# The output projection of a hybrid decoder layer as seven half products, with factors made in the merge

## The chip, the cores and the metric

The kernel runs on one core of a Trainium2 chip. Its work is done by TensorE (PE in the profile; PEld is its weight load), VectorE (DVE), ScalarE (ACT) and GpSimd (POOL); SyncE (SP) issues most DMAs. The metric is the time of one execution on the device in microseconds (us).

## The reference

One decoder layer over 512 tokens of width 1024: an mLSTM branch and a sliding-window attention branch read the same normalised input; their outputs are merged under gates, projected, and added to x. Then come an MLP and a gated embedding.

```
y_a = sigmoid(o_ml) * h_ml                     # mLSTM branch
y_b = swa_with_sinks(...)                      # attention branch
merged = sigmoid(g_a) * (y_a @ w_branch_a) + sigmoid(g_b) * (y_b @ w_branch_b)
x = x + merged @ w_out                         # the output projection
u = rmsnorm(x, norm_mlp_g) @ w_up
x = x + square(relu(u)) @ w_down
gate = sigmoid(rmsnorm(x, norm_ple_g) @ w_ple_gate)
x = x + gate * (p @ w_ple_proj)
return rmsnorm(x, final_norm_g)
```

All of it is in float32. The change concerns the line with w_out, the merge ahead of it, and the transposes of x behind it.

## The kernel before

A product of float32 matrices is made of three matmuls: each operand is split into a high part in a rounded format (fp32r) and the remainder, and high times high, high times low and low times high are summed in PSUM. `split` (L134 and L135) does it: ScalarE casts the high part, VectorE subtracts it from the operand to get the remainder. `load_w` loads 128x1024 of weights through SP (L143) and splits them into `wh` and `wl`. A matmul has 128 rows and columns of weights and 512 columns of moving data.

**The mLSTM branch ends** with four heads' value products (L784), which read the value tiles `vm`. `ya_of` multiplies a head's transposed outputs by the output gates, which `gate_of` loads from HBM by SP (`gl` from `god`, L619), and splits them into `ya`. The products of w_b with the attention branch run between; their results lie in `t2` (`gb` in the profile).

**The merge** has eight products of w_a with `ya`, one for each 128 channels and all 512 tokens, of 24 matmuls each. The results go to two PSUM tiles in turn (`psg`). VectorE multiplies each by its gate (L850, into `sga`), POOL adds the attention part (L851), and the sum is split into `mg`, high and low (L134, L135).

**The output projection** comes after the PSUM pools of the branches are closed and new ones opened. SP loads x there, four tiles of 128 tokens (`xk`, L864). For each half of the 1024 output columns, four chunks of w_out come in, and each is multiplied for four token tiles by six matmuls: 2 x 4 x 4 x 6 = 192, into `psp` and `psg`. After each half, VectorE adds the results to `xk` (L895), and `columns_of` transposes four columns of 128 of it (four 128x128 transposes on PE for each, L877) and splits them with the norm's gain (ScalarE L137, VectorE L138) into `x1`. Each column has a PSUM tile of two banks (`pair`) to itself, of which it uses one.

**Then** `up` multiplies w_up with `x1`, after ScalarE has begun to square `xk` for the norm (`junk`, L916). The down projection behind it already works by quarters: seven products in place of eight block products, from four quarters of the weights and of the activations and from sums of them.

The order of the work isn't the order of the program text: a scheduler places each instruction on its engine's queue ahead of time, and an engine runs its queue strictly in that order. A tile with several buffers hands out a slot again when its last user is done, and the next user waits for that.

## Time and profile before

| | us |
| --- | --- |
| three runs | 904.98, 906.15, 906.18 |
| median | 906.15 |
| the profiled execution | 905.84 |
| its span | 904.1 |
| PE busy | 890.4 |
| DVE busy | 627.0 |
| ACT busy | 466.9 |
| POOL busy | 28.1 |

Times in rows of the timeline count from the start of the span. A row gives start, length, engine, line, operation, the tile written and those read, the shape, and in brackets the engine's idle time ahead of it with what ended it. Where PE works without a gap, its row of two or more matmuls is as long as its modelled pipeline; the spacing of starts is what one costs. Against the span of 904.1, the whole execution has 1.74 us around it. The merge with w_a lies from 413 to 460, the output projection from 460 to 507 and `up` and `down` behind it.

### The profile page before, as it was taken

The page shows a single profiled execution, that of the slowest core. Times are in us where ns is not written, and L with a number is a line of the kernel's source. Part 1 is how long each engine was busy: PE and PEld are TensorE (multiplying, and loading weights), DVE is VectorE, ACT ScalarE, POOL GpSimd, SP SyncE. Part 2 cuts the span into 40 slices and gives each one's busy share as a digit, 9 for nine tenths or more (in the row PEclk, how much of TensorE's full clock was granted, in tenths as well). Part 3 has the DMA queues.
Part 4 walks back from the last instruction along what each step waited for, and adds up shares of the span by engine and source line. Part 5 has one row for each costly group of instructions (what it writes and reads, how often), then busy time and mean ns, then how long its engine had stood idle before and what let it go on. Part 6 is the DMA issues. An engine that isn't in the chain of part 4 may idle for free.

```text
span 904.1 us, 11781 instructions
## 1 busy us (share of the span) xinstructions
PE 890.4 (98%) x4500; PEld 741.6 (82%) x4500; DVE 627.0 (69%) x1016; ACT 466.9 (52%) x778; POOL 28.1 (3%) x47
## 2 busy tenths in 40 slices
PE   8999999999999999999999999999999999999996
PEld 7888899998877677777878888888888888888786
DVE  6884687874787977557644568856965795689556
ACT  6473444443676667664322555345535543554753
POOL 2021000000000000001210000000000000000000
PEclk9999999999999999999999999999999999999999
DMA  7753134435121132234452620631262044101402
GB/s 259 252 159 125 47 116 157 149 122 168 61 70 52 43 117 71 94 103 150 144 187 94 228 74 2 209 119 45 68 212 94 1 162 161 49 24 50 160 1 94
DMA packets 30347, 101.52 MB, mean 112 GB/s; under 512 B 4301, under 2 KB 4813, under 8 KB 30290
## 3 DMA queue, kind: packets, MB, share of 16 engines
q1 hardware_dynamic: 28002, 93.15, 31.0%
q0 software_dynamic: 2144, 7.35, 2.3%
q8 instruction: 35, 0.57, 0.3%
q10 hardware_dynamic: 144, 0.26, 0.1%
q14 instruction: 22, 0.18, 0.1%
HBM read 91.30 MB, written 8.40 MB: 110 GB/s over the span
## 4 chain that ended last, share of the span: by engine, by line
PE 73%; ACT 2%; DVE 2%; DMA 1%; issue 0%; SPq 0%; ACTq 0%
PE psg L162 42%; PE psp L162 22%; PE pst L784 2%; PE pst L713 1%; PE psa L705 1%; PE pst L774 1%; PE psa L162 1%; PE psa L668 1%; PE psa L669 1%; DMA gfin<-in_g_fin 1%; PE psp L877 1%; ACT jk L796 1%; ACT wh L134 1%; ACT pT L707 0%; DMA ptok<-in_p 0%
## 5 line engine op out<-in xcount | busy, mean ns | idle before, releaser
L135 DVE TENSOR_TENSOR wl<-wr,wh 128x1024 fp32r<-128x1024 f32 x134 | 170.7, 1279 | 131.0 <-ACT wh L134 124.4
L134 ACT CAST wh<-wr 128x1024 fp32r<-128x1024 f32 x134 | 140.9, 1053 | 208.5 <-PE psg L162 85.6
L162 PE MATMUL psg<-x,wh 128*128 128x512 f32 x512 | 157.9, 389 | 0.0
L162 PE MATMUL psp<-wh,uf 128*128 128x512 f32 x448 | 139.2, 390 | 0.0
L162 PEld LDWEIGHTS psg<-x,wh 128*128 128x128 f32 x512 | 96.0, 188 | 19.8
L162 PE MATMUL psg<-h,wh 128*128 128x512 f32 x320 | 101.3, 395 | 0.0
L162 PE MATMUL psg<-x,wl 128*128 128x512 f32 x256 | 99.6, 389 | 0.0
L162 PEld LDWEIGHTS psp<-wh,uf 128*128 128x128 f32 x448 | 84.1, 188 | 17.4
L162 PE MATMUL psp<-wl,uf 128*128 128x512 f32 x224 | 87.2, 390 | 0.0
L134 ACT CAST wh<-wd 128x1024 fp32r<-128x1024 f32 x44 | 46.3, 1055 | 60.4 <-PE psp L162 23.2
L162 PEld LDWEIGHTS psg<-h,wh 128*128 128x128 f32 x320 | 58.7, 188 | 15.9 <-issue 4.9
L135 DVE TENSOR_TENSOR wl<-wd,wh 128x1024 fp32r<-128x1024 f32 x44 | 53.3, 1220 | 17.6 <-ACT wh L134 17.4
L162 PE MATMUL psg<-h,wl 128*128 128x512 f32 x160 | 62.8, 393 | 0.0
L162 PEld LDWEIGHTS psg<-x,wl 128*128 128x128 f32 x256 | 48.1, 188 | 10.0
L162 PE MATMUL psa<-h,wh 128*128 128x256 f32 (+1 forms) x256 | 55.1, 311 | 0.2 <-ACT p L593 0.2
L162 PEld LDWEIGHTS psp<-wl,uf 128*128 128x128 f32 x224 | 42.0, 188 | 8.7
L135 DVE TENSOR_TENSOR uf<-F,uf 128x1792 fp32r<-128x1792 f32 (+2 forms) x20 | 33.0, 1652 | 21.8 <-ACT uf L134 21.8
L162 PEld LDWEIGHTS psa<-h,wh 128*128 128x128 f32 x256 | 41.8, 190 | 3.7 <-ACT p L593 0.9
L162 PE MATMUL psg<-yb,wh 128*128 128x512 f32 x128 | 42.7, 408 | 0.0
L162 PE MATMUL psg<-ya,wh 128*128 128x512 f32 x128 | 40.7, 394 | 0.0
L162 PE MATMUL psa<-h,wl 128*128 128x256 f32 (+1 forms) x128 | 39.6, 309 | 0.0
L134 ACT CAST uf<-F 128x1792 fp32r<-128x1792 f32 (+2 forms) x20 | 28.0, 1399 | 19.3 <-DVE F L951 19.2
(284 smaller groups left out, 1667.7 us busy)
## 6 DMA issues: line engine op xcount, KB each, us to landing
wr<-in_w_up SPq DMA_DIRECT2D x32, 512.0 KB, 3.2
wd<-in_w_down SPq DMA_DIRECT2D x24, 512.0 KB, 3.3
wr<-in_w_o SPq DMA_DIRECT2D x8, 512.0 KB, 4.8
gd<-gr POOLq DMA_DIRECT2D x8, 512.0 KB, 3.2
wr<-in_w_qsw SPq DMA_DIRECT2D x8, 512.0 KB, 4.0
wr<-in_w_qkml SPq DMA_DIRECT2D x8, 512.0 KB, 3.3
wr<-in_w_b SPq DMA_DIRECT2D x8, 512.0 KB, 3.2
gl<-gd SPq DMA_DIRECT2D x8, 512.0 KB, 3.4
```

The source lines that it names most:

```text
L134: A.copy(dst[0], src)
L135: V.tensor_sub(dst[1], src, r32(dst[0]))
L162: last_mm[0] = T.matmul(ps, l, r, start=first and i == 0, stop=last and i == len(ops) - 1, skip_group_check=parts)
L668: T.matmul(o, q[:, n * P : (n + 1) * P], kk[kp][ab][:, k0 : k0 + 256], start=True, stop=False)
L669: T.matmul(o, q[:, n * P : (n + 1) * P], kl[kp][ab][:, k0 : k0 + 256], start=False, stop=True)
L705: T.transpose(pt[:, c : c + P], lm3[ab][:, g, j * P : (j + 1) * P], ident)
L713: T.matmul(o[HALF[ab], :], vs[n + 1 - nk + j][:, c : c + 64], pTs[j][:, ab * 512 : (ab + 1) * 512], start=j == 0, stop=j == nk - 1,)
L774: T.matmul(psc[:, n0:], qk[4 + h][:, n0 : n0 + P], qk[h][:, n0:], start=True, stop=True)
L784: T.matmul(pn[:, : DV + 1], wT[s][:, t * P : (t + 1) * P], vm[s][:, h, :], start=s == 0, stop=s == t)
L796: A.activation(jk[:, :DV], h_of(h, t), AF.Square, scale=rd[:, t : t + 1], accum_out=hss[:, h, t : t + 1])
L877: T.transpose(ps[:, m * P : (m + 1) * P], xk[m][:, k * P : (k + 1) * P], ident)
```

## The change

The output projection is written as seven products of halves, as in the down projection. `merged` is seen as four blocks, two halves of the tokens by two halves of the channels of each pair; w_out as four quarters b11, b12, b21, b22. For each pair of merged results (the even one holds A21 and A11 as its two token halves, the odd one A22 and A12), the merge now makes the sums S1 = A21 + A22, S2 = S1 − A11, S3 = A11 − A21 and S4 = A12 − S2, and splits A11, A22 with A12, S1 with S2 and S3 with S4. Four sums of quarters are made in place (b12 from b22 and b12, and so on), each for both halves kh of the channels. Each product then has 24 matmuls: two token tiles, four pairs of channels in two halves, three matmuls each with 512 columns. X, Y and Z are PSUM tiles that take A11 and A12; S2, S3 and A22; S1 and S4. ScalarE copies X after A11 (`p1`). VectorE adds X, Y, Z and `p1` to `xk` as they are done, eighteen additions of 128x512 in place of eight.

The x tiles (`xk`) now take over the slots of the value tiles (tag `tk`, moved to a pool that lives on), and their loads are issued ahead of the merge. b11 and b12 lie in `lm`, b21 in `pT`, b22 in `wr`. The PSUM pools are closed only after the projection. `columns_of` takes its PSUM from the caller: `two_columns` puts two columns into one tile of two banks. The calls for columns 0 to 3 stand inside the last product (S4 with b22), those for 4 to 7 behind it. The host lays w_out out by quarters. The remaining code is the same; line numbers are higher by one before the change, and by 92 behind it.

On SP, where the last output gates are loaded (`gl`) ahead of the merge, before:

```order
L143 DMA wr_4301<-in_w_a 128x1024
L619 DMA gl_4032<-god_466 128x1024
L619 DMA gl_4052<-god_467 128x1024
L143 DMA wr_4341<-in_w_a 128x1024
L619 DMA gl_4098<-gd_1834 128x1024
```

and after:

```order
L144 DMA wr_4304<-in_w_a 128x1024
L144 DMA wr_4360<-in_w_a 128x1024
L859 DMA xk_4077<-in_x 128x1024
L859 DMA xk_4078<-in_x 128x1024
L859 DMA xk_4079<-in_x 128x1024
L859 DMA xk_4080<-in_x 128x1024
L620 DMA gl_4035<-god_469 128x1024
L620 DMA gl_4055<-god_470 128x1024
L144 DMA wr_4396<-in_w_a 128x1024
```

The four x loads and one load of w_a have moved ahead of the two gate loads.

On DVE, in the middle of the merge, two products' steps before (`sga` is a merged result, `gl` its gate, `wl` and `mg` are remainders):

```order
L850 TENSOR_TENSOR sga_4175<-psg_4144,gl_4176 128x512
L135 TENSOR_TENSOR wl_4304<-wr_4301,wh_4303 128x1024
L135 TENSOR_TENSOR mg_4181<-sga_4175,mg_4180 128x512
L850 TENSOR_TENSOR sga_4215<-psg_4184,gl_4176 128x512
L135 TENSOR_TENSOR wl_4344<-wr_4341,wh_4343 128x1024
L135 TENSOR_TENSOR mg_4219<-sga_4215,mg_4218 128x512
```

and after, behind the third product's multiplication (L865, sga_4208) and a sum of quarters (L932), up to the fifth's multiplication (`ms` are the sums S1 to S4, `wl_4466` the remainder of a quarter of w_out):

```order
L136 TENSOR_TENSOR mg_4156<-sga_4208,mg_4155 128x256
L865 TENSOR_TENSOR sga_4244<-psg_4213,gl_4209 128x512
L136 TENSOR_TENSOR wl_4399<-wr_4396,wh_4398 128x1024
L136 TENSOR_TENSOR mg_4250<-sga_4244,mg_4249 128x512
L887 TENSOR_TENSOR ms_4253<-sga_4208,sga_4244 128x256
L888 TENSOR_TENSOR ms_4253<-ms_4253,sga_4208 128x256
L136 TENSOR_TENSOR mg_4258<-ms_4253,mg_4257 128x512
L892 TENSOR_TENSOR ms_4254<-sga_4208 128x256
L893 TENSOR_TENSOR ms_4254<-sga_4244,ms_4253 128x256
L136 TENSOR_TENSOR wl_4466<-wq_4069,wh_4465 128x1024
L136 TENSOR_TENSOR mg_4264<-ms_4254,mg_4263 128x512
L865 TENSOR_TENSOR sga_4298<-psg_4267,gl_4299 128x512
```

From one pair's first multiplication to the next pair's there are thirteen steps in place of six.

On ACT, at the projection's end, before, with the last four columns of `x1` (`x_799` is its high part):

```order
L916 ACTIVATE junk_4712,ss_4713<-xk 128x1024
L916 ACTIVATE junk_4717,ss_4718<-xk 128x1024
L137 ACTIVATE x_799_4392<-psp_4675,gmlp 128x512
L137 ACTIVATE x_799_4392<-psp_4682,gmlp 128x512
L137 ACTIVATE x_799_4392<-psp_4689,gmlp 128x512
L916 ACTIVATE junk_4722,ss_4723<-xk 128x1024
L137 ACTIVATE x_799_4392<-psp_4696,gmlp 128x512
```

and after, with all eight (`x_831` is the high part, and of the tiles 4703 holds columns 0 and 1, 4723 columns 2 and 3, 4743 columns 4 and 5, 4756 columns 6 and 7):

```order
L138 ACTIVATE x_831_4457<-psa_4703,gmlp 128x512
L138 ACTIVATE x_831_4457<-psa_4723,gmlp 128x512
L138 ACTIVATE x_831_4457<-psa_4703,gmlp 128x512
L1008 ACTIVATE junk_4784,ss_4785<-xk_4077 128x1024
L138 ACTIVATE x_831_4457<-psa_4723,gmlp 128x512
L1008 ACTIVATE junk_4789,ss_4790<-xk_4078 128x1024
L138 ACTIVATE x_831_4457<-psa_4743,gmlp 128x512
L138 ACTIVATE x_831_4457<-psa_4756,gmlp 128x512
L1008 ACTIVATE junk_4794,ss_4795<-xk_4079 128x1024
```

The squares for the norm stand between the copies of the columns, and two columns of a tile are copied one after the other, with others between. On PE all 32 transposes now stand ahead of the first `up` matmul; before, the last four of them stood ten matmuls behind it.

The diff:

```diff
--- before.py
+++ after.py
@@ -77,6 +77,7 @@
     wp = pool(ctx, "wp")
     bp = pool(ctx, "bp")
     ap = pool(st_a, "ap")
+    xp = pool(ctx, "xp", side="right")
     c1 = pool(st_s, "c1", side="right")
     sp = pool(st_s, "sp", side="right")
     pp = pool(st_p, "pp", space=PSUM)
@@ -117,7 +118,7 @@
         return hl, [[t[:, k, :] for t in hl] for k in range(KT)]
 
     def tk(n):
-        return sp.tile([P, NH * (DV + 1)], F32, tag="tk", bufs=4, name=nm(n))
+        return xp.tile([P, NH * (DV + 1)], F32, tag="tk", bufs=4, name=nm(n))
 
     def tok_scratch(n="lm"):
         return sp.tile([P, D], F32, tag="lm", bufs=LMB, name=nm(n))
@@ -842,59 +843,150 @@
     ya_of(3)
 
 
-    mg = []
-    for i in range(8):
+
+
+    def load_quarter(c, pool_, tag, bufs):
+        t = pool_.tile([P, 1024], F32, tag=tag, bufs=bufs, name=nm("wq"))
+        nc.sync.dma_start(out=t, in_=w_out[c])
+        return t
+
+    b11 = [load_quarter(4 * kh, sp, "lm", LMB) for kh in range(2)]
+    b12 = [load_quarter(4 * kh + 1, sp, "lm", LMB) for kh in range(2)]
+
+
+    xk = [tk("xk")[:, :D] for _ in range(NT)]
+    for m in range(NT):
+        nc.sync.dma_start(out=xk[m], in_=x[m * P : (m + 1) * P, :])
+
+    def merged(i):
         ps = ps_g()
         mm_T(ps, load_w(w_a[i], KT * P, KT), ya)
         sg = act_f("sga")
         V.tensor_mul(sg, ps, gate_of(gad, i))
         G.tensor_tensor(sg, sg, t2[i], ALU.add)
-        m_ = act_hl("mg")
-        split(m_, sg)
-        mg.append(m_)
-
-
-    st_s.close()
-    st_p.close()
-    xp = pool(ctx, "xp", side="right")
-    pp = pool(ctx, "pq", space=PSUM)
-    XK = xp.tile([P, NT, D], F32, name="xk")
-    xk = [XK[:, m, :] for m in range(NT)]
-    for m in range(NT):
-        nc.sync.dma_start(out=xk[m], in_=x[m * P : (m + 1) * P, :])
-
-    def pair():
-
-        return pp.tile([P, 2, 512], F32, tag="pair", bufs=3, name=nm("psp"))
-
-    def ps_g():
-        return pp.tile([P, 512], F32, tag="g", bufs=2, name=nm("psg"))
-
-    def columns_of(dst, k, g):
-
-        ps = pair()[:, 0, :]
+        return sg
+
+    halves_of = lambda t: [t[:, :256], t[:, 256:]]
+
+    mf = []
+    for i in range(4):
+        even, odd = merged(2 * i), merged(2 * i + 1)
+        a21, a11 = halves_of(even)
+        a22, a12 = halves_of(odd)
+        if i % 2 == 0:
+            own = act_hl("mg")
+        part = [halves_of(t)[i % 2] for t in own]
+        split(part, a11)
+        f = {"A11": part}
+        hl = act_hl("mg")
+        split(hl, odd)
+        f["A22"], f["A12"] = zip(*[halves_of(t) for t in hl])
+        t12, t34 = act_f("ms"), act_f("ms")
+        s1, s2 = halves_of(t12)
+        s3, s4 = halves_of(t34)
+        V.tensor_add(s1, a21, a22)
+        V.tensor_sub(s2, s1, a11)
+        hl = act_hl("mg")
+        split(hl, t12)
+        f["S1"], f["S2"] = zip(*[halves_of(t) for t in hl])
+        V.tensor_sub(s3, a11, a21)
+        V.tensor_sub(s4, a12, s2)
+        hl = act_hl("mg")
+        split(hl, t34)
+        f["S3"], f["S4"] = zip(*[halves_of(t) for t in hl])
+        mf.append(f)
+
+    b22 = [load_quarter(4 * kh + 3, wp, "wr", WRB) for kh in range(2)]
+    b21 = [load_quarter(4 * kh + 2, sp, "pT", 2) for kh in range(2)]
+
+    def halves_a():
+        t = ps_a()
+        return [t[:, :512], t[:, 512:]]
+
+    def columns_of(dst, k, g, ps):
+
         for m in range(NT):
             T.transpose(ps[:, m * P : (m + 1) * P], xk[m][:, k * P : (k + 1) * P], ident)
         split(dst[k], ps, g[:, k : k + 1])
 
 
+    def out_proj():
+        X, Y, Z = halves_a(), halves_a(), [ps_t(), ps_t()]
+
+        def form(raw):
+            return load_w(None, 1024, 2, raw)
+
+        def prod(ps, a, w, kh, first, last, toks=range(2)):
+            for t in toks:
+                ops = []
+                for k in range(2):
+                    ops += pairs([h[:, t * P : (t + 1) * P] for h in mf[2 * kh + k][a]], [h[:, k, :] for h in w])
+                chain(ps[t], ops, first and kh == 0, last and kh == 1, True)
+
+        def acc(ps, toks, n, part=range(2)):
+            for t in part:
+                o = xk[2 * toks + t][:, n * 512 : (n + 1) * 512]
+                V.tensor_add(o, ps[t], o)
+
+        for kh in range(2):
+            V.tensor_sub(b12[kh], b22[kh], b12[kh])
+        for kh in range(2):
+            prod(X, "A11", form(b11[kh]), kh, True, False)
+            V.tensor_add(b11[kh], b12[kh], b11[kh])
+        own = [act_f("p1") for _ in range(2)]
+        for t in range(2):
+            A.copy(own[t], X[t])
+        for kh in range(2):
+            prod(Y, "S2", form(b11[kh]), kh, True, False)
+        acc(Y, 1, 1)
+        for kh in range(2):
+            prod(X, "A12", form(b21[kh]), kh, False, True)
+            V.tensor_sub(b21[kh], b21[kh], b11[kh])
+        acc(X, 1, 0)
+        for kh in range(2):
+            prod(Y, "S3", form(b12[kh]), kh, False, False)
+        acc(Y, 0, 1)
+        acc(own, 0, 1)
+        for kh in range(2):
+            V.tensor_sub(b11[kh], b22[kh], b11[kh])
+            prod(Z, "S1", form(b11[kh]), kh, True, False)
+        acc(Z, 0, 1)
+        acc(own, 1, 1)
+        acc(own, 0, 0)
+        for kh in range(2):
+            prod(Y, "A22", form(b21[kh]), kh, False, True)
+        acc(Y, 0, 0)
+
+        w = [form(b22[kh]) for kh in range(2)]
+        prod(Z, "S4", w[0], 0, False, True)
+        two_columns(0)
+        prod(Z, "S4", w[1], 1, False, True, [0])
+        acc(Z, 1, 1, [0])
+        two_columns(2)
+        prod(Z, "S4", w[1], 1, False, True, [1])
+        acc(Z, 1, 1, [1])
+        two_columns(4)
+        two_columns(6)
+
     x1b, x1 = big_hl("x1")
-    for nh in range(2):
-        if nh == 0:
-            a, b = pair(), pair()
-            pv = [a[:, 0, :], a[:, 1, :], b[:, 0, :], b[:, 1, :]]
-        else:
-            a = pair()
-            pv = [a[:, 0, :], a[:, 1, :], ps_g(), ps_g()]
-        for c in range(4):
-            w = load_w(w_out[nh * 4 + c], 2 * 512, 2)
-            for m in range(NT):
-                mm_tok(pv[m], w, mg[2 * c : 2 * c + 2], m, first=c == 0, last=c == 3)
-        for m in range(NT):
-            o = xk[m][:, nh * 512 : (nh + 1) * 512]
-            V.tensor_add(o, pv[m], o)
-        for k in range(4):
-            columns_of(x1, 4 * nh + k, gmlp)
+
+    def two_columns(k):
+        two = halves_a()
+        for i in range(2):
+            columns_of(x1, k + i, gmlp, two[i])
+
+    out_proj()
+
+    st_s.close()
+    st_p.close()
+    pp = pool(ctx, "pq", space=PSUM)
+
+    def pair():
+
+        return pp.tile([P, 2, 512], F32, tag="pair", bufs=3, name=nm("psp"))
+
+    def ps_g():
+        return pp.tile([P, 512], F32, tag="g", bufs=2, name=nm("psg"))
 
 
 
@@ -1056,10 +1148,10 @@
 
     x2b, x2 = big_hl("x2")
     for k in range(4):
-        columns_of(x2, k, gple)
+        columns_of(x2, k, gple, pair()[:, 0, :])
     ple(0, wp0)
     for k in range(4, 8):
-        columns_of(x2, k, gple)
+        columns_of(x2, k, gple, pair()[:, 0, :])
     evicted = ple(1, load_w(w_pp[1], 2 * 512, 2))
     rk = []
     fs = cp.tile([P, NT, 4], F32, name="fs")
@@ -1208,7 +1300,7 @@
         "w_gb": _halves(w[:, 5640:6664]),
         "w_a": _t_form(i["w_branch_a"][0]),
         "w_b": _t_form(_heads(i["w_branch_b"][0].T).T),
-        "w_out": _tok_form(i["w_out"][0], 2, 512),
+        "w_out": _quarters(i["w_out"][0]),
         "w_up": _t_form(i["w_up"][0]),
         "w_down": np.concatenate([_quarters(down[q * 1024 : (q + 1) * 1024]) for q in range(4)], axis=0),
         "w_pg": _tok_form(i["w_ple_gate"][0], 2, 512),
```

More of the change, by code (lines that the diff above doesn't have):

```diff
@@ new lines, in block_kernel @@
+    b22 = [load_quarter(4 * kh + 3, wp, "wr", WRB) for kh in range(2)]
[4 more added lines that the diff above has]
+    def columns_of(dst, k, g, ps):
+        for m in range(NT):
+            T.transpose(ps[:, m * P : (m + 1) * P], xk[m][:, k * P : (k + 1) * P], ident)
+        split(dst[k], ps, g[:, k : k + 1])
+    def out_proj():
[50 more added lines that the diff above has]
+        two_columns(6)
```

5 lines of the change are left out of this document (1 added, 4 removed).

## The prediction

> **What bounds the kernel now.** I read the engines and the chain of waits on the profile's page first, then busy time by stage, then PE's timeline where the stages meet. The page:
>
> ```profile
> span 904.1 us, 11781 instructions
> PE 890.4 (98%) x4500; PEld 741.6 (82%) x4500; DVE 627.0 (69%) x1016; ACT 466.9 (52%) x778; POOL 28.1 (3%) x47
> PE 73%; ACT 2%; DVE 2%; DMA 1%; issue 0%; SPq 0%; ACTq 0%
> ```
>
> PE is busy 98% of the span and holds most of the chain. The three stages below are the merge, the output projection and a stretch of the down projection, which already has seven products (columns: stretch, its length, then busy time of PE, PEld, DVE, ACT, POOL, granted clock, DMA share, GB/s).
>
> ```profile
> 413.00:460.30 47.30, 46.26 (x211) 37.38 (x208) 34.17 (x36) 16.70 (x22) 9.93 (x7) 1.00 0.48 156
> 460.30:507.00 46.70, 46.63 (x216) 38.31 (x216) 19.54 (x22) 11.99 (x16) 1.29 (x1) 1.00 0.41 145
> 551.00:590.00 39.00, 39.00 (x174) 32.30 (x173) 32.28 (x35) 18.76 (x20) 0.00 (x0) 1.00 0.40 135
> ```
>
> All three are PE's. In the projection VectorE (DVE) has more than half its time free; in the merge it is taken for 34 of 47 us. The clock is 1.00 throughout. PE around the projection:
>
> ```profile
> 460.37 0.47 PE L162 MATMUL psp<-wh,mg 128*128 128x512 f32 x1 [0.88 <-ACT wh L134]
> ...
> 461.60 0.62 PE L162 MATMUL psp<-wh,mg 128*128 128x512 f32 x2
> 462.28 0.62 PE L162 MATMUL psp<-wh,mg 128*128 128x512 f32 x2
> ...
> 506.08 1.60 PE L877 MATMUL psp<-ident,xk 128*128 128x128 f32 x12
> 507.44 0.71 PE L162 MATMUL psg<-x,wh 128*128 128x512 f32 x2
> ```
>
> Three matmuls take 462.28 − 461.60 = 0.68 us, so one 0.2267. PE waits 0.88 us once, at the stage's start, and nowhere at its end: twelve transposes from 506.08 to 507.44 (0.113 each) and the first up product follows.
>
> **The change, part by part.**
>
> *Fewer products.* 192 matmuls become 7 × 24 = 168 of the same shape: −24 × 0.2267 = −5.44 us. All of it is on PE, which is the path.
>
> *PSUM not reopened.* The 0.88 us wait is put down to the weight cast, but the first projection matmul writes PSUM tiles that only exist once the old pools are closed, and the last reader of those is the multiplication at 459.53 (below), which ends at 460.22. Now the pools stay open until the projection is over and the first product needs only early factors: −0.88.
>
> *The merge has more VectorE work.* Its steps now, by DVE and POOL:
>
> ```profile
> 423.69 0.69 DVE L850 TENSOR_TENSOR sga<-psg,gl 128x512 f32<-128x512 f32 x1 [0.86 <-PE psg L162]
> 424.55 2.36 DVE L135 TENSOR_TENSOR wl<-wr,wh 128x1024 fp32r<-128x1024 f32 x1 [0.16 <-ACT wh L134]
> 426.83 0.68 DVE L135 TENSOR_TENSOR mg<-sga,mg 128x512 fp32r<-128x512 f32 x1
> 427.43 0.68 DVE L850 TENSOR_TENSOR sga<-psg,gl 128x512 f32<-128x512 f32 x1
> 428.03 1.21 DVE L135 TENSOR_TENSOR wl<-wr,wh 128x1024 fp32r<-128x1024 f32 x1
> ...
> 459.53 0.69 DVE L850 TENSOR_TENSOR sga<-psg,gl 128x512 f32<-128x512 f32 x1 [1.65 <-PE psg L162]
> ```
> ```profile
> 424.54 1.29 POOL L851 TENSOR_TENSOR sga<-sga,gb 128x512 f32<-128x512 f32 x1 [216.55 <-ACT wh L134]
> 428.19 2.20 POOL L851 TENSOR_TENSOR sga<-sga,gb 128x512 f32<-128x512 f32 x1 [2.37 <-DVE sga L850]
> ```
> ```profile
> 553.80 0.42 DVE L948 TENSOR_TENSOR F<-F 128x256 f32<-128x256 f32 x1
> 554.26 0.42 DVE L950 TENSOR_TENSOR F<-F 128x256 f32<-128x256 f32 x1
> 558.23 1.22 DVE L997 TENSOR_TENSOR wd<-wd,wd 128x1024 f32<-128x1024 f32 x1
> 559.36 1.22 DVE L135 TENSOR_TENSOR wl<-wr,wh 128x1024 fp32r<-128x1024 f32 x1
> ```
>
> Two things are read here. Steps in a row cost about 0.09 less than they last: 0.60 for 128x512 (427.43 to 428.03), 1.13 for 128x1024 (558.23 to 559.36); so 0.34 for 128x256, and 0.46 where one uses the other's result. And the POOL addition and a VectorE step on two SBUF inputs don't run together: the later one is held for all of the other (2.36 instead of 1.22 at 424.55, 2.20 instead of 1.29 at 428.19). The Trainium skill, page "SBUF — State Buffer", section "SBUF: two separate sides", says the same more strictly: the port pair that VectorE and GpSimd share is an exclusive lock, held for the whole instruction by whichever came first. These rows agree with it; by that rule the sum is the one below, and without it some 3.8 us less.
>
> A product of 24 matmuls takes PE 5.44 us, a pair 10.88. Of a pair VectorE has before two multiplications, two weight remainders and two merge remainders: 2 × (0.60 + 1.13 + 0.60) = 4.7. Now it has two multiplications 1.20, three remainders of factors on 512 columns 1.80 and one on 256 0.34, four sums 1.60, two weight remainders 2.26 and a sum of quarters 1.13: 8.3. Three holes lie between them, since the steps stand in one fixed order: after each multiplication the remainder needs the POOL addition (which is held behind a 1024-wide step) and then ScalarE's cast, about 1.6 and 2.0 us after what VectorE has to do meanwhile, and S1/S2 need a cast, 0.8. That makes 12.8 a pair against PE's 10.88. The first pair, with both weight remainders held by POOL as at 424.55, brings the third multiplication to about 436.7 instead of 432.3 (459.53 − 5 × 5.44) and the fifth, 12.8 later, to 449.3. Product six (counted from zero) writes the PSUM tile that the fifth multiplication reads, of two; its turn on PE comes two products ahead of the last multiplication, at 459.53 − 2 × 5.44 = 448.65 less the 0.2 from its last matmul, and it gets the tile at 449.9 to 450.1: +1.5. Bounds: 0 if the holes fill, 3.9 if the second pair loses 4.3 like the first and not 1.9.
>
> *Waits inside the projection.* VectorE's work there is fourteen remainders of weights (three of them up's) and four sums of quarters, 18 × 1.13 = 20.3, sixteen accumulations into x, 9.6, the last pair's steps, 4.9, and a first column, 0.7: 35.5 of about 41 us, against 19.54 of 46.7 in the row above. Queue order then decides. (a) S2's second half needs the last pair's S2 remainder, which stands behind one more weight remainder. PE gets there at 450.0 + 10.88 + 5.44 (A11) + 2.72 (S2's first half) + 1.13 (five matmuls) = 470.2; VectorE multiplies for the last pair at about 461.2, and from there to the end of that remainder its steps and holes are 9.6: 470.8, +0.6. (b) A12 writes the tile that ScalarE copies first; both copies stand behind a weight cast and a factor's cast: +0.7. (c) S3's first weight remainder: +0.15. (d) A22's weight remainder stands behind eight accumulations, 8 × 0.60 = 4.8 us, of the 5.44 that the product ahead of it lasts: +0.8. Together +2.3. The down stage with its 32.28 of 39.00 has no PE wait, so the lower bound is 0; the upper one is 5, where the 35.5 us get the holes of a merge pair, 4.4, twice and not once.
>
> *The left columns.* x1's 32 transposes now write two columns into one two-bank tile, and all of them stand ahead of up; four columns are done inside the last product.
>
> ```profile
> 487.18 0.75 DVE L138 SCALAR_TENSOR_TENSOR x<-psp,gmlp,x 128x512 fp32r<-128x512 f32 x1 [0.15 <-ACT x L137]
> ...
> 505.60 1.06 ACT L916 ACTIVATE junk<-xk 128x1024 f32<-128x1024 f32 x1 [3.70 <-PE psg L162]
> 506.66 1.04 ACT L916 ACTIVATE junk<-xk 128x1024 f32<-128x1024 f32 x1
> 507.70 1.82 ACT L137 ACTIVATE x<-psp,gmlp 128x512 fp32r<-128x512 f32 x3
> 510.47 0.69 ACT L137 ACTIVATE x<-psp,gmlp 128x512 fp32r<-128x512 f32 x1
> ```
>
> The second column's transposes wait for the split of the first in the same tile; columns 4 and 6 wait for those of 1 and 3. ScalarE's order at the end is copies of 0, 2, 1, square, 3, square, 4, 6, square, 5, square, 7. The last transposes (column 7) need column 6 split. From the start of copy 1: copies 0.57 × 3 = 1.71 ((1.82 − 0.69)/2 each), two squares 2.12, the last copy 0.69, a handover 0.15, VectorE's 0.75, a handover 0.1: 5.5 us. PE has in that time two matmuls and 16 transposes, 0.45 + 1.8 = 2.25. So it waits 3.3 in all, in pieces of about one us; +3.4 with the other handovers. Bounds: 1.1 without the squares between, 4.4 if the third square comes ahead as well. What the up products are late by is not caught up later, since nothing behind them waits on anything but PE.
>
> *x earlier.* The four x loads move ahead of two gate loads in SP's queue, and can start only when the value tiles were last read:
>
> ```profile
> 403.82 3.30 PE L784 MATMUL pst<-vm,dm 128*128 128x257 f32 x14 [0.17 <-DVE hd L788]
> ```
> ```profile
> 413.48 1.64 SPq L619 DMA_DIRECT2D gl<-god  x2
> ...
> 460.25 1.75 SPq L864 DMA_DIRECT2D xk<-in_x  x4
> ```
> ```profile
> 411.00:414.00 3.00, 2.94 (x17) 2.17 (x16) 2.64 (x8) 1.31 (x2) 0.00 (x0) 1.00 0.00 0
> 414.00:417.00 3.00, 2.84 (x17) 2.44 (x18) 3.00 (x5) 1.24 (x2) 0.00 (x0) 1.00 0.73 213
> 462.00:464.00 2.00, 2.00 (x10) 1.65 (x10) 1.34 (x2) 0.31 (x1) 0.00 (x0) 1.00 1.00 383
> ```
>
> The values are free at 407.1. 2.1 MB at the 383 GB/s of the last row take 5.5 us, and first bytes come about 1.5 us after the issue (460.25 against 462): done at 414.2. The gate loads are issued at 413.48 in both kernels, their bytes due at 415.0: 0, covered by DMA engines that are idle (share 0.00) up to there. The spare is 0.8 us. The quarters' early loads lie in tiles that are free by then and likewise cost nothing; if they were late, the first sum of quarters would be, on VectorE.
>
> **Sum.** −5.44 − 0.88 + 1.5 + 2.3 + 3.4 = +0.9 on the profiled run's 905.84 (span 904.1), so 906.7. That run is 0.3 below the median of the three, 906.15.
>
> **Rivals.** Less than 0.2% (1.8 us) can't be told from no change here, so up to 904.3 counts as faster and from 908.0 as slower.
>
> *VectorE keeps up* (ends faster). POOL's additions fall between VectorE's two-input steps instead of on them, the fifth multiplication is done by 448.5 and the waits a to d go with it; only the end stays: 905.84 − 5.44 − 0.88 + 3.4 = 902.9. For it: the down stage carries 32 of 39 without a wait. Against: the rows at 424.55 and 428.19; and a product now leaves VectorE 5.44 − 0.69 − 2.36 − 0.68 = 1.7, which the new work, (8.3 − 4.7)/2 = 1.8, fills without the holes.
>
> *x delays the gates* (ends slower). If the four loads run at the 213 GB/s of 414 to 417 instead of 383, they take 9.8 us, end at 418.5, and the output gates for the last heads, ya and the merge come 3.5 later: 910.2. It decides once the loads end after 415.0. Against: 213 has 1 to 1.5 us of start-up in it.
>
> *No overlap of VectorE's steps* (ends slower). If a step costs its whole duration whenever it waits for the one before, two pairs of 13 steps lose 26 × 0.09 = 2.3 more by product six, and 0.8 more by A22: 909.8. For it: the factor sums use each other, 0.46 instead of 0.34. Against: 0.60 and 1.13 in the rows, between different tiles.
>
> **How the numbers follow.** My sum has chance 0.50, with a range of its own of 903.7 to 909.7: the bounds of the three plus terms together give 900.6 (0 + 0 + 1.1) and 912.8 (3.9 + 5 + 4.4), and I go halfway. 0.05 of it is faster, 0.36 within, 0.09 slower. VectorE keeps up: 0.22, faster. x delays the gates: 0.10, slower. No overlap: 0.15, of which 0.02 within. The 0.03 left are slower (several waits at once). So faster 0.27, same 0.38, slower 0.35. The range 902.3 to 910.0 leaves out about a third of the first rival (below), two thirds of the second and a quarter of the third: 0.07 + 0.07 + 0.04.
>
> **What would show it.** The number of projection matmuls falls by 24 and no wait of 0.88 is left at the first; a wait of PE on the multiplication (L865) at about 448.5, of 1.5 us; POOL additions of 2.2 to 2.3; waits of 0.6 to 0.8 at 470, 473 and 490; some 3 us of waits in the transposes (L909) ahead of up; gate loads at 413.5 as before; and up to down as long as now. I am wrong if PE doesn't wait on L865 in the merge, if the waits in the transposes add up to under 1.5 or over 4.5, or if the first sy multiplication moves.

## The result

| | us |
| --- | --- |
| the kernel before, 22 runs beside the changed one | 905.67 (904.38 to 906.69) |
| the changed kernel, 22 runs | 907.45 (904.75 to 909.06) |
| ratio | 1.0018, 95% interval 1.0011 to 1.0025 |
| the changed kernel's profiled execution | 907.43, span 905.7 |

The change makes the kernel slower by 0.18%, some 1.8 us, just inside what the prediction called no change, and 0.75 us above its 906.7. An eighth of the projection's matmuls, 24 of 192 or 5.4 us of PE time, is gone, and all of it and a little more is given back.

The page of the changed kernel says where: PE has 4.4 us less to do, VectorE 26.6 us more, and PE's share of the chain of waits falls from 73% to 66% while VectorE's rises from 2% to 6%.

```profile
span 905.7 us, 11804 instructions
PE 886.0 (98%) x4476; PEld 736.1 (81%) x4476; DVE 653.6 (72%) x1064; ACT 476.5 (53%) x794; POOL 31.4 (3%) x47
PE 66%; DVE 6%; ACT 3%; DMA 1%; issue 1%; POOL 1%; POOLq 0%; ACTq 0%; SPq 0%; DVEq 0%
```

The chain of waits of the stretch from 407 to 515 us, by line, of the kernel before and then of the changed one:

```profile
by line: PE psg L162 56.5%; PE psp L162 30.6%; PE psp L877 3.5%; ACT jk L796 2.3%; PE pst L824 1.8%; DVE hs L805 1.0%; ACT wh L134 1.0%; DVE sy L825 0.7%; issue 0.5%; DVE gb L814 0.4%; ACT hs L787 0.4%; ACT sd L274 0.3%; PE pst L784 0.2%; D
```
```profile
by line: DVE wl L136 14.4%; PE psg L163 11.7%; DVE mg L136 7.4%; DVE xk L929 6.2%; POOL sga L866 5.2%; PE psa L163 5.1%; PE pst L163 4.7%; issue 4.3%; DMA gl<-god 4.0%; ACT mg L135 3.7%; DVE sga L865 3.5%; PE psa L909 2.5%; ACT jk L797 2.3%
```

Before, the path runs almost wholly through PE. After, it leaves PE in the merge and runs through weight remainders (`wl`), merge remainders (`mg`), accumulations into x (`xk`) and POOL's additions, up to the product A22.

PE's timeline of the changed kernel shows every place at which it waits for them, and the start of `up`:

```profile
450.99 0.70 PE L163 MATMUL psg<-ya,wh 128*128 128x512 f32 x2 [1.44 <-DVE sga L865]
...
471.81 0.74 PE L163 MATMUL psa<-wh,mg 128*128 128x512 f32 x2 [0.35 <-DVE mg L136]
...
474.16 0.50 PE L163 MATMUL psa<-wh,mg 128*128 128x512 f32 x1 [0.44 <-ACT p L938]
...
491.73 0.50 PE L163 MATMUL psa<-wl,mg 128*128 128x512 f32 x1 [0.60 <-DVE wl L136]
...
503.76 0.40 PE L163 MATMUL pst<-wh,mg 128*128 128x512 f32 x1
...
505.69 0.63 PE L909 MATMUL psa<-ident,xk 128*128 128x128 f32 x4 [0.74 <-DVE ss L1009]
506.87 0.66 PE L909 MATMUL psa<-ident,xk 128*128 128x128 f32 x4 [0.55 <-DVE x L139]
508.49 1.32 PE L909 MATMUL psa<-ident,xk 128*128 128x128 f32 x8 [0.96 <-DVE x L139]
509.56 0.71 PE L163 MATMUL psg<-x,wh 128*128 128x512 f32 x2
```

The idle times in brackets count from the end of the modelled pipeline; by starts each wait is some 0.16 us longer (the first one is 450.99 − 449.16 − 0.23 = 1.60, where 449.16 is the matmul ahead). From the last projection matmul at 503.76 to `up` at 509.56 there are 5.8 us, of which twenty transposes and the last matmul account for 20 x 0.113 + 0.23 = 2.5: 3.3 us of waits.

VectorE's timeline of the merge has the three holes, and POOL's the additions that are held:

```profile
437.52 0.68 DVE L865 TENSOR_TENSOR sga<-psg,gl 128x512 f32<-128x512 f32 x1
...
440.96 0.42 DVE L136 TENSOR_TENSOR mg<-sga,mg 128x256 fp32r<-128x256 f32 x1 [1.62 <-ACT mg L135]
...
444.97 0.69 DVE L136 TENSOR_TENSOR mg<-sga,mg 128x512 fp32r<-128x512 f32 x1 [1.84 <-ACT mg L135]
...
447.15 0.69 DVE L136 TENSOR_TENSOR mg<-ms,mg 128x512 fp32r<-128x512 f32 x1 [0.69 <-ACT mg L135]
...
450.16 0.68 DVE L865 TENSOR_TENSOR sga<-psg,gl 128x512 f32<-128x512 f32 x1
```
```profile
438.35 2.13 POOL L866 TENSOR_TENSOR sga<-sga,gb 128x512 f32<-128x512 f32 x1 [8.48 <-DVE sga L865]
442.12 2.16 POOL L866 TENSOR_TENSOR sga<-sga,gb 128x512 f32<-128x512 f32 x1 [1.64 <-DVE sga L865]
```

A pair takes VectorE 450.16 − 437.52 = 12.64 us. And one wait that the sum had put at nothing, in SP's and VectorE's rows:

```profile
406.24 1.75 SPq L859 DMA_DIRECT2D xk<-in_x  x4
413.81 0.33 SPq L620 DMA_DIRECT2D gl<-god  x1
```
```profile
418.24 1.41 DVE L826 SCALAR_TENSOR_TENSOR sy<-pst,gml,gl 128x512 f32<-128x512 f32 x2 [0.81 <-DMA gl<-god]
```

The same multiplication began at 417.01 in the kernel before, without a wait.

Between marks that both traces have, the account is this (marks: the first product with `ya`, the merge's first multiplication, the first projection matmul, the first `up` product, the first `down` product):

| stretch | before | after | difference |
| --- | --- | --- | --- |
| first `ya` product to first multiplication | 10.70 | 11.27 | +0.57 |
| to the first projection matmul | 36.68 | 37.35 | +0.67 |
| to `up` | 47.07 | 47.58 | +0.51 |
| to `down` | 44.14 | 43.62 | −0.52 |
| together | 138.59 | 139.82 | +1.23 |

The spans differ by 1.6 us; 0.37 of it lies ahead of the first mark. Most of the −0.52 in the last row is no gain: in the kernel before four of the 32 transposes stand inside `up`, after the change all stand ahead of it, 4 x 0.113 = 0.45.

### The profile page after: what moved, and what is told of

Its sections match the earlier page's. It is cut to its first block, busy times and chain, and to the rows that moved or that the text cites. A ratio compares the mean times of both kernels' runs of the same rounds, so it can differ in the third digit from the quotient of the medians.

```text
span 905.7 us, 11804 instructions
## 1 busy us (share of the span) xinstructions
PE 886.0 (98%) x4476; PEld 736.1 (81%) x4476; DVE 653.6 (72%) x1064; ACT 476.5 (53%) x794; POOL 31.4 (3%) x47
## 4 chain that ended last, share of the span: by engine, by line
PE 66%; DVE 6%; ACT 3%; DMA 1%; issue 1%; POOL 1%; POOLq 0%; ACTq 0%; SPq 0%; DVEq 0%
PE psg L163 37%; PE psp L163 19%; PE pst L785 2%; DVE wl L136 2%; PE psa L163 2%; PE pst L714 1%; PE psa L706 1%; PE pst L775 1%; PE psa L669 1%; DVE mg L136 1%; PE psa L670 1%; DMA gfin<-in_g_fin 1%; DVE xk L929 1%; POOL sga L866 1%; PE pst L163 1%
## 5 line engine op out<-in xcount | busy, mean ns | idle before, releaser
L136 DVE TENSOR_TENSOR wl<-wr,wh 128x1024 fp32r<-128x1024 f32 x126 | 155.4, 1238 | 109.0 <-ACT wh L135 99.0
L135 ACT CAST wh<-wr 128x1024 fp32r<-128x1024 f32 x126 | 132.2, 1051 | 177.2 <-PE psg L163 65.4
L135 ACT CAST wh<-wq 128x1024 fp32r<-128x1024 f32 x26 | 27.1, 1051 | 22.6 <-PE psg L163 9.1
```

Of the source, the lines that this page charges most:

```text
L135: A.copy(dst[0], src)
L136: V.tensor_sub(dst[1], src, r32(dst[0]))
```

## The experiments

The times that follow are compared, by ratio, with runs of the kernel before that were taken beside them on the same chip. The stretches are those of the table above, each from one trace; the first row of that table, in which most edits change nothing, scatters by some tenths of a us.

**x loaded later.** The loads of x move behind the first two loads of merge gates (`loaded[1]` is the last gate load issued so far).

```diff
-            nc.sync.dma_start(out=loaded[0], in_=put[i // 2])
+            loaded[1] = nc.sync.dma_start(out=loaded[0], in_=put[i // 2])
...
-    for m in range(NT):
-        nc.sync.dma_start(out=xk[m], in_=x[m * P : (m + 1) * P, :])
...
     for i in range(4):
         even, odd = merged(2 * i), merged(2 * i + 1)
...
+        if i == 1:
+            with tc.issue_after(loaded[1].ins):
+                for m in range(NT):
+                    nc.sync.dma_start(out=xk[m], in_=x[m * P : (m + 1) * P, :])
```

> The four x loads are issued behind the last output gates and the first merge gates, not ahead of them; nothing else moves. Theory: in the changed kernel the x transfers make the output gates late, so the sy multiplication at 418.24 waits 0.81 us for a DMA and the merge begins 0.6 us later; VectorE holds the chain from there on and passes it to the end. So 0.4 to 0.8 us less than the changed kernel, about 906.8, and no DMA wait ahead of L826. Rival: the gates' lateness is hidden behind VectorE's backlog, no change, 907.4.

Measured: 907.5 us, ratio 1.0014 (1.0002 to 1.0026) against the changed kernel's 1.0018: not told apart by the times. The trace tells it. The wait for the DMA is gone:

```profile
416.65 1.40 DVE L826 SCALAR_TENSOR_TENSOR sy<-pst,gml,gl 128x512 f32<-128x512 f32 x2
```

The first stretch takes 10.50 us in place of 11.27, the rest is unchanged (37.32, 47.55, 43.64), and the way from the first `ya` product to `down` is 139.01 in place of 139.82. So between these two traces the loads cost 0.8 us at that place and it comes through to `down`. It isn't so in each execution. Of the seven traces here with the x loads ahead of the gates five have the wait, of 0.35 to 0.81 us, and two don't (the sums later, both columns first); their first stretch is 10.69 to 11.28, 11.06 on average. The four traces without the loads there have 10.50 to 10.94, 10.74 on average. By that the loads cost about 0.3 us, which the medians of these runs can't show.

**The addition on VectorE.**

```diff
-        G.tensor_tensor(sg, sg, t2[i], ALU.add)
+        V.tensor_add(sg, sg, t2[i])
```

> The addition of the attention part in the merge is done by VectorE instead of POOL. Theory: what costs in the merge is not VectorE's work but the holes that POOL's additions make (held behind a 1024-wide step, and VectorE waiting for them): eight additions of 0.60 us more on VectorE, and yet the wait on L865 at 450.99 (1.44 us) goes and those at 471.8 and 491.7 shrink; 2 to 3 us less than the changed kernel, about 904.9. Rival: VectorE simply has too much to do, 4.8 us more makes the waits longer: 1 to 3 us more, about 909.

Measured: 906.9 us, ratio 1.0012 (1.0003 to 1.0021), between the two. The wait on L865 had not gone but moved to the product before:

```profile
434.38 1.23 DVE L932 TENSOR_TENSOR wq<-wq,wq 128x1024 f32<-128x1024 f32 x1 [2.50 <-DMA wq<-in_w_out]
```
```profile
439.36 0.70 PE L163 MATMUL psg<-ya,wh 128*128 128x512 f32 x2 [1.93 <-DVE sga L865]
```

A sum of quarters had been put earlier on VectorE's queue and waited there for its quarter's load, and the multiplication stood behind it. So the next run takes that away. This trace holds a second cost, of another kind: from 506.38 to 509.78 PE's granted clock was at 0.50, with PE busy throughout, which costs 1.7 us (columns below as in the prediction; more on this at the end). The last eight transposes and the start of `up` lie in it, and from `up` to `down` it is 44.54 us in place of 43.62.

```profile
506.38:509.78 3.40, 3.40 (x13) 3.01 (x14) 1.93 (x6) 3.07 (x7) 0.00 (x0) 0.50 0.95 352
```

**The same, with the sums of quarters later.** The sums for b12 stay behind the sixth multiplication.

```diff
-        V.tensor_mul(sg, ps, gate_of(gad, i))
-        G.tensor_tensor(sg, sg, t2[i], ALU.add)
+        muls.append(V.tensor_mul(sg, ps, gate_of(gad, i)))
+        V.tensor_add(sg, sg, t2[i])
...
-        for kh in range(2):
-            V.tensor_sub(b12[kh], b22[kh], b12[kh])
+        with tc.issue_after(muls[5].ins):
+            for kh in range(2):
+                V.tensor_sub(b12[kh], b22[kh], b12[kh])
```

> As the run with the addition on VectorE, but the two sums of quarters for b12 are held back on VectorE's queue until the sixth multiplication of the merge; in that run one of them had been put early and waited 2.50 us for its quarter's load, with the multiplication behind it. Theory: POOL's holes were the cost in the merge, and only that load hid the gain: no PE wait of over 0.5 us from the merge to the product S4, 3 to 3.5 us less than the changed kernel, about 0.9980 of the kernel before. Rival: VectorE is full, and the sums, now later, make the waits behind A11 longer: as the changed kernel, 1.0018.

Measured: 905.21 us, ratio 0.9993 (0.9981 to 1.0006). In the trace the theory holds: no wait on the merge's multiplication at all (L867 here), and of the waits inside the projection only one of 0.21 is left. VectorE's rows of one pair, from multiplication to multiplication:

```profile
434.02 0.68 DVE L867 TENSOR_TENSOR sga<-psg,gl 128x512 f32<-128x512 f32 x1
...
436.86 0.69 DVE L867 TENSOR_TENSOR sga<-psg,gl 128x512 f32<-128x512 f32 x1 [0.52 <-PE psg L163]
...
444.96 0.68 DVE L867 TENSOR_TENSOR sga<-psg,gl 128x512 f32<-128x512 f32 x1
```

A pair takes 444.96 − 434.02 = 10.94 us in place of 12.64, which is PE's own pace, and VectorE waits for PE once. A sum of quarters, 1.13, has left this stretch and two additions, 1.2, have come in, so VectorE's work is the same; what is gone are the holes of 1.62 and 1.84 (0.47 is left of the first, nothing of the second). That rests on the rows: no run held the sums back with the addition left on POOL, so the runs alone don't part the two edits. The way to `down` is 135.59, 4.2 less than in the changed kernel. Of this 0.6 lies in the first stretch, where the edit changes nothing and the gate load happened to be in time; 3.6 is the edit's. The profiled execution took 902.34; the median of twelve runs shows only 2.2 us less than the changed kernel.

**Both columns of a tile first.**

```diff
         two = halves_a()
         for i in range(2):
-            columns_of(x1, k + i, gmlp, two[i])
+            for m in range(NT):
+                T.transpose(two[i][:, m * P : (m + 1) * P], xk[m][:, (k + i) * P : (k + i + 1) * P], ident)
+        for i in range(2):
+            split(x1[k + i], two[i], gmlp[:, k + i : k + i + 1])
```

> The eight transposes of both columns of a PSUM tile come first, then both splits, so no transpose waits for the split of its tile's other column. Theory: the waits ahead of the up products (3.4 us in all) come from the two columns that share a tile: 1.0 to 1.5 us less than the changed kernel, about 906.2. Rival, the prediction's words: they come from the squares that stand between the copies on ScalarE, which stay: within 0.3 us of the changed kernel.

Measured: 906.16 us, ratio 1.0004 (0.9995 to 1.0013): 1.3 us less than the changed kernel, at the place and of the size that the theory says, though the two intervals overlap a little. PE's waits at the end are one of 0.15 and

```profile
504.07 0.77 PE L977 MATMUL psa<-ident,xk 128*128 128x128 f32 x5 [0.64 <-DVE ss L1012]
505.10 1.07 PE L977 MATMUL psa<-ident,xk 128*128 128x128 f32 x8 [0.26 <-DVE x L139]
511.92 0.50 PE L163 MATMUL psg<-x,wh 128*128 128x512 f32 x1 [0.74 <-DVE x L139]
```

The last one is `up` itself, which runs into a column that isn't split yet. From the first projection matmul to `down` the way is 45.72 + 44.67 = 90.39 in place of 91.20, so 0.8 of the 1.3 comes from here; in the first stretch, which the edit leaves alone, it was 0.4.

**Without the squares.**

```diff
-        A.activation(junk, xk[m], AF.Square, accum_out=ss)
-        V.tensor_scalar(ss, ss, 1.0 / D, EPS, ALU.mult, ALU.add)
+        V.tensor_scalar(ss, xk[m][:, :1], 1.0 / D, EPS, ALU.mult, ALU.add)
```

> The changed kernel without the four squares for the norm (one value of x stands in for the sum, so the output isn't the layer's). The prediction's words: two squares of 1.06 us stand in the chain of the last columns, so up begins 2.1 us earlier, about 1.0 us less than the kernel before less what stands in their place. Rival: the chain is that of the columns sharing a tile, transposes to copy to remainder to transposes, and the squares fill its gaps: up begins within 0.5 us of the changed kernel.

Measured: 909.87 us, ratio 1.0041 (1.0027 to 1.0055). `up` doesn't begin earlier: 48.06 us from the first projection matmul in place of 47.58. But the run didn't free what it was to free. Where a square stood, ScalarE now casts the next weights (1.04 us from 504.51), and VectorE's remainder of them comes to stand in the chain of waits ahead of the last transposes (rows of the chain: start, length, what it ran through):

```profile
505.74 1.13 DVE wl L136
...
507.58 0.67 PE psa L909 x4
...
508.28 0.70 ACT x L138
...
509.00 0.76 DVE x L139
...
509.81 0.66 PE psa L909 x4
```

PE's waits there are 0.75, 1.07 and 0.91 in place of 0.74, 0.55 and 0.96. Behind the remainder a ring lies open, transposes, copy, remainder and transposes again, through tiles that two columns share, and ScalarE's copies wait for PE in it (0.42 and 1.04). So something else of that length is there to take the squares' place; that the squares cost nothing isn't shown. In the changed kernel the chain of waits runs through two of them, one behind the other with the copies:

```profile
503.73 0.56 ACT x L138
...
504.31 1.14 ACT junk L1008 x2
505.45 0.58 ACT x L138
506.03 1.03 ACT junk L1008 x2
507.07 0.59 ACT x L138
...
507.68 0.76 DVE x L139
...
508.49 0.66 PE psa L909 x4
...
509.14 0.66 PE psa L909 x4
```

The run is some 2 us slower than the changed kernel. In its trace 0.5 of that lies in the stretches of the table, and 1.7 behind `down`'s start. There, behind two waits of 1.15 and 0.60 at transposes far from the change, PE's clock was at half from 848.48 to 851.89, which accounts for the 1.7:

```profile
848.48:851.89 3.41, 3.41 (x13) 2.82 (x12) 2.93 (x5) 2.31 (x3) 0.00 (x0) 0.50 0.01 2
```

**Without the product S3.** Its 24 matmuls are left out; the weights are split all the same.

```diff
         for kh in range(2):
-            prod(Y, "S3", form(b12[kh]), kh, False, False)
+            form(b12[kh])
```

> The 24 matmuls of the product S3 are left out, so the output is not the layer's; all its factors, weights, sums and accumulations stay. Theory: from the merge to the product A22 VectorE, not PE, sets the time: PE only waits longer ahead of A22 (some 5.8 us in place of 0.60), and the time falls by less than 1 us. Rival: PE is the path and its waits are a matter of a us here and there: 24 x 0.2267 = 5.4 us less, about 902.

Measured: 908.55 us, ratio 1.0030 (1.0017 to 1.0044): with 5.4 us of PE's work taken away the kernel is no faster, and rather 1 us slower than the changed one. The way from the first projection matmul to `up` is 48.67 in place of 47.58. PE's row, and busy time, granted clock and DMA of the stretches around it (columns as in the prediction):

```profile
484.52 0.79 PE L163 MATMUL pst<-wl,mg 128*128 128x512 f32 x1 [5.46 <-DVE wl L136]
```
```profile
478.40:484.50 6.10, 0.66 (x3) 0.20 (x2) 6.10 (x10) 0.00 (x0) 0.00 (x0) 0.76 0.00 0
484.50:488.50 4.00, 3.98 (x10) 3.16 (x11) 4.00 (x5) 2.81 (x3) 0.00 (x0) 0.51 0.00 0
```

The theory's wait is there, 5.46 where 5.8 was expected, and VectorE is busy for all 6.10 us of it: it sets the time. But the loss has a second cause. After the wait PE works at half its clock for 4 us (0.51 in the second row; ten matmuls there, against fifteen in the 3 us behind it at 1.00), which costs 2 us. Without that the way to `up` would be some 46.7, 0.9 less than in the changed kernel; this is an estimate. The Trainium skill, page "TensorE: Matmul & The Clock Gate", section "Part 1: The HAM clock gate (the "warmup" mystery)", says that an idle window of about 3.4 us halves the clock and that about as long a busy one restores it. This trace agrees in the main, with 5.46 us idle and about 4 us of slow work, but the clock fell at 481.58 already, some 2.5 us into the wait.

**Without half of S3.** The control for that, meant to keep each wait too short for the clock to fall.

```diff
-            prod(Y, "S3", form(b12[kh]), kh, False, False)
+            prod(Y, "S3", form(b12[kh]), kh, False, False, [0])
```

> The changed kernel without half of the product S3 (12 matmuls, one of the two token tiles), so the output isn't the layer's; all factors, weights, sums and accumulations stay. Leaving out all 24 had made one PE wait of 5.46 us, after which PE ran at half its clock for about 4 us. Theory: VectorE sets the time there, so with half of them no wait is long enough for the clock to fall, and the way from the first projection matmul to the first up product still gets no shorter, within 0.7 us of the changed kernel's 47.58. Rival: without the clock's fall leaving out work pays, 12 x 0.2267 = 2.7 us less there, 44.9.

Measured: 908.89 us, ratio 1.0044 (1.0021 to 1.0068). The way to `up` is 48.33, 0.75 longer than in the changed kernel, a little outside the 0.7 expected, and far from the rival's 44.9. PE waits in three pieces on VectorE, and the clock stays at 1.00 though PE is busy for 1.20 of 4 us:

```profile
489.93 0.47 PE L163 MATMUL pst<-wh,mg 128*128 128x512 f32 x1 [1.24 <-DVE xk L929]
491.04 0.49 PE L163 MATMUL pst<-wh,mg 128*128 128x512 f32 x1 [0.64 <-DVE xk L929]
492.77 0.50 PE L163 MATMUL psa<-wl,mg 128*128 128x512 f32 x1 [1.24 <-DVE wl L136]
```
```profile
489.00:493.00 4.00, 1.20 (x3) 0.60 (x4) 4.00 (x7) 0.54 (x1) 0.00 (x0) 1.00 0.00 0
```

So up to A22 PE's work isn't what counts. That it is even slower, by 0.75, goes with the order of VectorE's queue, which the scheduler wrote anew here (two accumulations stand ahead of A22's weights that stood behind them); that part was not tested by itself.

**The kernel before with its PSUM pools kept.** Of the change only this: the projection uses tiles of the old pools, which are closed behind it.

```diff
     st_s.close()
-    st_p.close()
     xp = pool(ctx, "xp", side="right")
-    pp = pool(ctx, "pq", space=PSUM)
...
-            a, b = pair(), pair()
+            a, b = ps_a(), ps_a()
...
-            columns_of(x1, 4 * nh + k, gmlp)
+            columns_of(x1, 4 * nh + k, gmlp, ps_a()[:, :512] if (nh, k) == (1, 2) else ps_t())
+
+    st_p.close()
+    pp = pool(ctx, "pq", space=PSUM)
```

> The kernel before with one part of the change alone: the PSUM pools are closed behind the output projection, which uses their tiles; everything else stays, x loads and eight block products too. Theory: PE's wait of 0.88 us at the first projection matmul is the reopening of PSUM, not the weight cast it is put down to; it goes, and the reopening now stands ahead of the first up product, where it waits for the last columns to be read, 1.5 to 2 us: 0.5 to 1 us slower than the kernel before. Rival: the cast is what it waits for, the 0.88 stays at its place.

Measured: 906.51 us, ratio 1.0010 (1.0001 to 1.0019). One of the eleven executions took 3148.51 us, which nothing here explains; the ratio leaves it out. The first half of the theory holds, the second doesn't. PE's first projection matmul and its row ahead of `up`:

```profile
459.96 0.39 PE L162 MATMUL psa<-wh,mg 128*128 128x512 f32 x1
...
508.65 0.66 PE L867 MATMUL pst<-ident,xk 128*128 128x128 f32 x4 [1.52 <-DVE x L138]
```

The 0.88 is gone (35.62 in the second stretch in place of 36.68), so it was the reopening of PSUM and not the cast that the row named: a cast begins 0.20 us behind the last merge matmul in both traces (459.30 and 459.10 before, 459.93 and 459.73 here), and here PE doesn't wait for it. The new wait of 1.52 isn't a reopening: it stands at a column's transposes and waits for the split of an earlier column, behind a square (1.23) and a copy in the chain of waits. By the diff fewer tiles were given to the columns here; that this is the reason wasn't tested by itself.

**All together.** The addition on VectorE with the sums later, x later, both columns first, and the squares held behind the last column's copy:

```diff
-            A.activation(dst[0], src, AF.Copy, scale=scale)
+            last_copy[0] = A.activation(dst[0], src, AF.Copy, scale=scale)
...
-        A.activation(junk, xk[m], AF.Square, accum_out=ss)
+        with tc.issue_after(last_copy[0].ins):
+            A.activation(junk, xk[m], AF.Square, accum_out=ss)
```

> The addition on VectorE with the sums held back, x loaded behind the first merge gates, both columns of a tile transposed first, and the squares behind the last column's copy. Theory: the four costs lie one behind the other on the path and their gains add up: 0.6 + 3.3 + 1.3 less than the changed kernel, some 5 us, about 0.996 of the kernel before. Rival: they overlap, since a later stage's backlog takes up what an earlier one gives back: 2.5 to 3 us less than the changed kernel, about 0.999.

Measured: 902.92 us (901.17 to 903.44), ratio 0.9963 (0.9951 to 0.9976): 3.3 us faster than the kernel before and 5 faster than the changed one, the size that the theory says; the rival's 0.999 is outside the interval. PE's waits in the projection and behind it are

```profile
501.69 0.77 PE L983 MATMUL psa<-ident,xk 128*128 128x128 f32 x5 [0.65 <-DVE xk L934]
503.57 1.06 PE L983 MATMUL psa<-ident,xk 128*128 128x128 f32 x8 [1.12 <-DVE x L141]
```

and two of 0.15 and 0.21, the latter for the copies `p1`. The four stretches are 10.94, 35.61, 44.59 and 43.64, 134.78 together in place of 138.59. The first is no shorter than in the run with the addition on VectorE and the sums later (10.69), which loads x early: the later x shows no gain here. The columns and the squares do: 1.1 us less from the first projection matmul to `up` than that run's 45.65, with nothing lost in `up`. What the squares alone give wasn't run.

## Why the prediction was right, and where it wasn't

It forecast 906.7 by a sum of gains and losses of about the same size, and 907.45 came out. Term by term, from the starts in the trace:

- **Fewer products, −5.44.** The 24 matmuls are gone and those left take 0.2267 as before. Without S3 another 24 were left out and the way to `up` was no shorter (0.9 us with the clock's loss taken off, as an estimate), which shows that these 5.44 are only worth what VectorE leaves of them.
- **PSUM not reopened, −0.88.** Shown by the pools alone. By starts it was 460.37 − 459.10 − 0.23 = 1.04.
- **The merge, +1.5.** 1.60 by starts, at the place forecast, for the reason forecast: a pair takes VectorE 12.64 against 12.8, with holes of 1.62, 1.84 and 0.69 against 1.6, 2.0 and 0.8. With the additions off POOL and the two sums held back, the holes and the wait were gone.
- **Waits inside the projection, +2.3.** By starts 0.51, 0.61, none and 0.76, together 1.9 against 0.6, 0.7, 0.15 and 0.8.
- **The left columns, +3.4.** 3.3, and the working holds in the changed kernel's trace: from the start of copy 1 (503.73) to the last column's transposes (509.14) it is 5.41 us against 5.5, through the copies and the two squares that the sum lists. Its lower bound, 1.1 without the squares between, remains open: in the run without squares a weight cast and its remainder took their place. The shared tile belongs to the chain too, since with both columns transposed first PE's waits ahead of `up` were 0.15, 0.64 and 0.26.
- **x earlier, 0.** This is the step that was wrong in the sum: "done at 414.2". The four x loads were issued from 406.24 to 407.62 and landed 4.6, 7.4, 8.2 and 8.9 us later, the last at 416.5, past the 415.0 that the prediction itself had set as the limit. The sum had them move at 383 GB/s from the start; but a load of w_a went ahead of them (0.5 MB, which the kernel before moves between 405 and 409), and from 409 to 411 the rate was only 225 to 234. The first gate load, issued at 413.81, took 4.34 us to land, in the kernel before 3.1, and VectorE waited 0.81 for it. That is 0.57 in the first stretch of this trace, and some 0.3 by all traces. The sign "if the first sy multiplication moves" looked at the wrong one: the first stood where it was within the shift of the traces (413.70, before 413.36), the third waited. The rival with this name had the mechanism, and its condition came true; at 3.5 us it had the wrong size.

The terms as measured give −5.44 − 1.04 + 1.60 + 1.9 + 3.3 + 0.57 = +0.9, the marks +1.23; the 0.3 between them isn't assigned. What the medians show beyond that, 1.8 against 1.2, isn't assigned either. That the total came out within 1 us of 906.7 is in part luck: the waits inside the projection came out 0.4 lower than forecast and x 0.6 higher.

Of the rivals, "VectorE keeps up" became true once POOL's additions were on VectorE and the two sums held back: its condition, that the additions fall between VectorE's steps, was the one that failed. "No overlap of VectorE's steps" is excluded by the rows: 0.60 and 1.14 from step to step in the changed kernel too (437.52 to 438.12, 450.76 to 451.90).

## What to carry to other kernels

A form that saves PE an eighth of its matmuls and pays with sums on another engine is worth its price only while that engine has time left in each period of PE's work; count that engine's steps per period with the holes that its fixed order makes, not by its mean share. An addition put on an idle engine can cost more than on the busy one, when the two hold each other up (2.13 us for an addition of 1.29) and the busy one waits for the result. Two columns in one PSUM tile are better both written before either is read; that was worth some 0.8 us here. A run without an operation shows what the operation costs only if nothing else moves into its place: look at the chain of waits of both runs.

## What was unexpected in the hardware

- PE's granted clock fell to 0.50 for 3.41 us, or for twice that, and came back: from 481.58 to 488.41 without S3, from 506.38 to 509.78 with the addition on VectorE, from 848.48 to 851.89 without the squares, and from 12.81 to 16.22 in the changed kernel, ahead of all that was changed. Where PE works throughout, that costs 1.7 us. In the 3.41 us ahead of the falls PE was busy for 0.89, 1.34, 1.66 and 1.75 us. Only the first has a long wait (5.46 us); in the second and the third none in brackets is over 1.15. Nor do short waits always lower it: without half of S3, PE was busy for 1.20 of 4 us with waits of 1.24, 0.64 and 1.24, and in the changed kernel for 1.30 of the 3.40 us from 505.10, both at 1.00. What decides between them wasn't tested.
- Executions of two of the kernels spread with the granted clock of the whole run: in the run with the addition on VectorE and the sums later, the four with 0.998 took 902.34 to 903.14 us, the eight with 0.993 to 0.997 took 904.57 to 908.20. The changed kernel's five with 0.995 took 907.67 to 909.06, its nine with 0.999 904.75 to 907.66. One fall of 1.7 us in some 905 is 0.002 of that clock, so 0.993 may be three of them; this is an estimate, since only one execution of each kernel has a trace. The five executions of the kernel with all changes don't follow it (901.17 at 0.995, 901.79 at 0.999).
- A load issued at the same place took 4.3 us in place of 3.1 to land (the first of the two gate loads, issued at 413.81 and 413.48) when 2 MB had gone ahead of it, of which the last half landed at 415.3 and 416.5.
